# Start addresses of the weight tiles chosen by matmul width, and the gate block's low part of every second inner tile made by an adding transfer

## The chip, the cores and the metric

One core of one Trainium2 chip runs the whole program. The metric is device time in microseconds, lower is better; the time of a kernel is the median of its runs. A core has a matmul engine, TensorE (PE in the profile; its weight loads are PEld), three elementwise engines, VectorE (DVE), ScalarE (ACT) and GpSimd (POOL), and SyncE (SP), which here only issues transfers. GpSimd issues transfers too, among them the adding ones, whose data are added to what stands in SBUF.

## The reference

A two-layer streaming encoder on 512 frames of width 1024. Layer 0 mixes by an RWKV-7 scan, layer 1 by chunked attention; both attend to 256 memory tokens beside it, project, and end in a gated convolution block, which is where most of the change lies:

```python
def conv_glu(h, w_in, conv_w, conv_b, w_out):
    seq = h.shape[1]
    gate, val = jnp.split(h @ w_in, 2, axis=-1)          # 1024 -> 2 x 2816
    gp = jnp.pad(gate, ((0, 0), (CONV_W - 1, 0), (0, 0)))
    conv = conv_b + sum(conv_w[j] * gp[:, j:j + seq] for j in range(CONV_W))
    return (jax.nn.gelu(conv, approximate=False) * val) @ w_out

for layer in range(2):
    ...
    mo = memory_attention(q_mem, mem_n, w_mem_kv[layer])
    x = x + jnp.concatenate([mix, mo], axis=-1) @ w_out[layer]
    x = x + conv_glu(rms_norm(x, ln2[layer]), ffn_in[layer], ffn_conv[layer],
                     ffn_conv_b[layer], ffn_out[layer])
return rms_norm(x, ln_f)
```

## The kernel before

**Three matmuls for one product.** Each float32 operand is held as two parts of type float32r: a high part (a cast by ScalarE, `whi` for weights) and a low part (`wlo`, what the cast left off). A product is high by high, high by low and low by high. The low part of a weight tile comes in one of two ways: VectorE subtracts the high part from the raw weights, or ScalarE writes the negated raw weights and GpSimd issues an adding transfer that brings the weights in a second time. In that second way what is added in memory to minus the rounded copy is the weight, so the low part remains.

**Wide and narrow matmuls.** In the projections (`dense`, L221, L222, L225) the activations `r1h`, `r1l`, `r2h`, `r2l` are the moving operand, 512 columns at a time, and `whi` or `wlo` is loaded as 128x128 weights. In the output step of the gated block (`rows`, L658, L663) it is the other way round: slices of the activations are loaded and 512 columns of `whi` or `wlo` move. Both are called wide here. In the frames of the gated block (`prod`, L414, L416), and in the value projection of layer 1 (L1724 to L1726), 256 columns move: narrow.

**The frames.** The gated block's input product is done by seven block products in place of eight (Winograd's form of Strassen's scheme). There are 22 inner tiles of 128 columns (j). The tiles 0 to 20 are objects of the class `Seven`, one `frame` each, and tile 21 is done plainly in `ending`. A frame issues 7 calls of `prod`, each with 4 blocks of 3 matmuls: 84 narrow matmuls. Three calls use the normed activations (`XU`: r2h, r2l in layer 0, r1h, r1l in layer 1), four use sums of them (`XT`: th, tl in both layers). Weights of a frame are seven blocks of a raw tile, two raw tiles alternating: `load` fetches four (G1, V1, G2, V2), VectorE makes sums (`sums` L455, `sum2` L460, `sum4` L464). ScalarE casts four high parts a frame (`high`, L468), VectorE subtracts three low parts (`lower`, L473: two of 1024 columns, one of 512), and the low part of G2 and V2 comes by an adding transfer (`rest`, L450 and L451). The gate block G1 with S2 is the first operand of a frame (`gs`); its two parts are made in the frame before. Besides, VectorE and ScalarE end the tiles before (`end1` to `end5`), and GpSimd issues one adding transfer of the convolution (`endd`, L491). `keep` fixes the order of all of these on VectorE and ScalarE as it is written.

**Where tiles lie.** Tiles of the pool `wp` have 1024 words a partition. `whi` and `wlo` have three buffers each, in rotation. By the built program's allocations, in bytes from the start of a partition:

| tile | before | before, mod 128 | after | after, mod 128 |
|---|---|---|---|---|
| whi, three buffers | 66176, 70272, 74368 | 0 | 66560, 75008, 83456 plus 0 (wide) or 64 (narrow) | 0 or 64 |
| wlo, three buffers | 78464, 82560, 86656 | 0 | 70784, 79232, 87680 plus 128 (wide) or 64 (narrow) | 0 or 64 |
| r1h, r1l | 20640, 37024 | 32 | 20736, 37120 | 0 |
| r2h, r2l | 107136, 123520 | 0 | 108288, 124672 | 0 |
| th, tl | 152192, 168576 | 0 | 153344, 169728 | 0 |

Every operand of a wide or narrow matmul begins at a multiple of 512 bytes from its tile's start, so the last figure of a tile holds for all its slices. In what follows, the place of a matmul is the distance, mod 128 bytes, between the moving operand's start and the start of the weights that are loaded while it moves. Counted over the built order of float32r matmuls that follow one another (512 columns or 256):

| place | wide, before | wide, after | narrow, before | narrow, after |
|---|---|---|---|---|
| 0 | 1151 | 2256 | 2835 | 79 |
| 32 or 96 | 1140 | 36 | 1214 | 185 |
| 64 | 5 | 5 | 0 | 3785 |

Of the kernel before, what the change touches and what calls it, by code (L numbers as in the profile page):

```python
# [10 lines left out]
F32 = mybir.dt.float32  # L11
F32R = mybir.dt.float32r
AF = mybir.ActivationFunctionType
# [5 lines left out]
P = 128  # L19
S = 512  # L20
# [93 lines left out]


@with_exitstack
def trunk_kernel(ctx, tc, A, out):
# [19 lines left out]
    rc = cp.tile([P, 4], F32, name="rc")  # L137

# [32 lines left out]

    def split_w(raw, n, src=None, pin=lambda i: i, first=False, hold=False):
        hi = wp.tile([P, 1024], F32R, name="whi", tag="whi")
        lo = wp.tile([P, 1024], F32R, name="wlo", tag="wlo")
# [12 lines left out]
        if hold:  # L187
            return hi, lo, second
        second()
        return hi, lo  # L190

    def raw_w(src, n=1024):
        raw = wp.tile([P, 1024], F32, name="wraw", tag="wraw", bufs=2)
        raw_at[0] = nc.sync.dma_start(raw[:, :n], src)
        return raw[:, :n]

    def load_w(src, n=1024, lo=None):
        return split_w(raw_w(src, n), n, src if (lo_on[0] if lo is None else lo) else None)

# [30 lines left out]
    def run(g):  # L230
        for y in g:
            assert not callable(y) or y()
# [164 lines left out]
    def ffn(l, hp, U, T, new_x, xT, after=None, tokens=None):  # L397
# [22 lines left out]
        def keep(ins):  # L420
            return tc.keep_in_program_order(ins) if pinned[0] else ins
# [5 lines left out]
        class Seven:  # L427

            def __init__(self, j):
                self.j = j  # L430

# [34 lines left out]
            def high(self, what, n=1024):  # L466
                hi = wp.tile([P, 1024], F32R, name="whi", tag="whi")
                keep(SC.copy(hi[:, :n], self.pair(what) if n > S else self.raw[:, what]))  # L468
                return hi

            def lower(self, what, hi, n=1024):
                lo = wp.tile([P, 1024], F32R, name="wlo", tag="wlo")
                keep(V.tensor_tensor(lo[:, :n], self.pair(what) if n > S else self.raw[:, what], hi[:, :n], op=ALU.subtract))  # L473
                return hi, lo
# [31 lines left out]
            def frame(self, prev2, prev, nxt, norm=None, ending=None):  # L506
                first = prev is None
                if nxt:
                    nxt.load()
# [3 lines left out]
                if first:  # L513
                    hv = self.hv
                    self.h31 = self.high(S3)
                else:
                    hv = self.high(G2)
                keep(SC.copy(g[:, h1], f1[:, h1]))
                if first:
# [359 lines left out]
    def flat(t, n):  # L879

        return t[:].rearrange("p a b c -> p (a b c)").rearrange("p (m s) -> p m s", m=n)
# [4 lines left out]
    def lora_load(idx):  # L886
        raw = wp.tile([P, 1024], F32, name="wraw", tag="wraw", bufs=2)
        nc.sync.dma_start(raw[:], A["lora"][idx])
        return raw
# [5 lines left out]
    xs += [flat(kt_("AR", (P, NCH, 2, 64), bufs=2), 2) for _ in range(2)]  # L895
    lraw = wp.tile([P, 1024], F32, name="wraw", tag="wraw", bufs=2)
    for m in range(KD):
# [4 lines left out]
    nc.sync.dma_start(vec[:, 24:], A["vec"][:, 24:])  # L902
    kraw = wp.tile([P, 1024], F32, name="wraw", tag="wraw", bufs=2)
    nc.sync.dma_start(kraw[:], A["wA"][1])
# [16 lines left out]
    def lora_split(idx, raw, parts=1):  # L921

        hi, lo = zip(*((wp.tile([P, 1024], F32R, name="whi", tag="whi"), wp.tile([P, 1024], F32R, name="wlo", tag="wlo"))
                       for _ in range(2)))
        mraw = flat(kt_("KB", (P, NCH, 3, 64), bufs=2), 1)[:, 0, 0:1024]
        r3 = raw[:].rearrange("p (k f) -> p k f", k=8)
# [566 lines left out]
    def lora_one():  # L1493

        with tc.issue_after(norm_at[0].ins):
            *_, lw_ = lora_split(1, lora_load(1))
        yield from lora_pair(1, *lw_)


# [8 lines left out]
    GP.memset(acc[:, 0:S:64], 0.0)  # L1508
    run(lora0)
    first = prepare(0, Ts[0])  # L1510
    for _ in range(5):
# [131 lines left out]
    with ExitStack() as bctx:  # L1643
# [153 lines left out]
        run(dense(pk[:], [(wk, K8)], act1, order=K8[4:8], start=False))  # L1797
        wv = [load_w(A["w_kvv"][0, u]) for u in range(2)]
        run(norm)
# [189 lines left out]
```

## Time and profile before

| | us |
|---|---|
| median of 3 runs | 1302.26 (1301.45 to 1303.33) |
| profiled execution, its time | 1301.85 |
| profiled execution, its span | 1300.1 |
| ten steady frames of layer 0 (one matmul to the same matmul ten frames on) | 100.80 |
| ten steady frames of layer 1 | 100.00 |

The span is the time from the first to the last instruction; what lies around it is 1.75 us. The granted TensorE clock was 0.998 of full speed. In the profile's rows an engine, a line of the kernel, an operation, out<-in by tile names and a count stand first, then busy time and the mean duration of one. Matmuls overlap: a row of 283 ns each in a stream that starts one every 0.12 us means that the next starts long before the end of the last. Where all matmuls of a stream are alike, a difference between two rows' mean durations is a difference between their start-to-start times as well.

### The profile page before, as it was taken

To read this page: it belongs to the slowest core of one execution; us is meant where nothing else is said; L and a number is where in the kernel's file an instruction comes from. 1 tells how busy PE (TensorE), PEld (TensorE's weight loads), DVE (VectorE), ACT (ScalarE), POOL (GpSimd) and SP (SyncE) were. 2 spreads that over 40 slices of the span, in tenths; PEclk is the share of its full clock that TensorE was granted. 3 is DMA by queue.
4 is the path that set the end of the run, shared out by engine and by line. 5 is a ranking of instruction groups with operands and counts; after the bars stand their busy time and mean duration, and the time that the engine had idled before them with its cause. 6 is when DMAs were issued, how large, how long until landed. Compare 5 with 4: busy or idle time off the path is not lost.

```text
span 1300.1 us, 26329 instructions
## 1 busy us (share of the span) xinstructions
PE 1278.6 (98%) x10420; PEld 1100.9 (85%) x10420; DVE 1041.8 (80%) x1956; ACT 836.5 (64%) x1380; POOL 137.6 (11%) x164
## 2 busy tenths in 40 slices
PE   9999999999999999999999999999999999999997
PEld 7887777777789999999888878787799999998886
DVE  7967767775589999999876876658889999998684
ACT  6666767756566666767554676657757666665562
POOL 1000000000001112110220000000011122111200
PEclk9999999999999999999999999999999999999999
DMA  6365434452236777886984332223437878879951
GB/s 202 110 177 116 112 69 106 95 113 69 82 114 148 182 175 193 189 183 176 270 179 122 123 90 85 81 95 115 130 80 183 183 173 197 186 159 285 214 141 65
DMA packets 92988, 187.42 MB, mean 144 GB/s; under 512 B 21824, under 2 KB 30144, under 8 KB 92864
## 3 DMA queue, kind: packets, MB, share of 16 engines
q1 hardware_dynamic: 68592, 129.14, 31.1%
q0 software_dynamic: 24272, 56.59, 25.0%
q8 instruction: 82, 1.34, 0.4%
q14 instruction: 42, 0.34, 0.1%
HBM read 169.48 MB, written 6.29 MB: 135 GB/s over the span
## 4 chain that ended last, share of the span: by engine, by line
PE 83%; DVE 7%; ACT 6%; issue 1%; DMA 1%; SPq 0%; ACTq 0%; DVEq 0%
PE psf L414 21%; PE psf L416 11%; PE psf L658 7%; PE psd L225 6%; PE psd L221 6%; PE psd L222 5%; PE psf L663 4%; PE psd L658 3%; PE psd L663 2%; PE pss L1774 1%; PE pss L658 1%; DVE wlo L183 1%; PE pss L1404 1%; PE pss L350 1%; PE pss L1760 1%
## 5 line engine op out<-in xcount | busy, mean ns | idle before, releaser
L468 ACT CAST whi<-raw 128x1024 fp32r<-128x1024 f32 (+1 forms) x168 | 151.8, 941 | 66.2 <-PE psf L414 37.4
L414 PE MATMUL psf<-tl,whi 128*128 128x256 f32 x672 | 168.6, 283 | 0.0
L414 PE MATMUL psf<-th,whi 128*128 128x256 f32 x672 | 168.3, 283 | 0.0
L473 DVE TENSOR_TENSOR wlo<-raw,whi 128x1024 fp32r<-128x1024 f32 (+1 forms) x126 | 131.5, 1043 | 14.3 <-ACT whi L468 14.2
L175 ACT CAST whi<-wraw 128x1024 fp32r<-128x1024 f32 x84 | 87.7, 1047 | 69.3 <-PE psd L222 36.1
L414 PEld LDWEIGHTS psf<-tl,whi 128*128 128x128 f32 x672 | 128.7, 192 | 0.0
L414 PEld LDWEIGHTS psf<-th,whi 128*128 128x128 f32 x672 | 128.5, 192 | 0.0
L221 PE MATMUL psd<-r1h,whi 128*128 128x512 f32 x264 | 108.2, 410 | 0.0
L222 PE MATMUL psd<-r1l,whi 128*128 128x512 f32 x264 | 105.6, 401 | 0.0
L183 DVE TENSOR_TENSOR wlo<-wraw,whi 128x1024 fp32r<-128x1024 f32 x65 | 79.3, 1219 | 15.9 <-ACT whi L175 13.6
L648 ACT CAST whi<-raw 128x1024 fp32r<-128x1024 f32 (+1 forms) x52 | 49.6, 954 | 65.2 <-PE psf L658 35.4
L649 DVE TENSOR_TENSOR wlo<-raw,whi 128x1024 fp32r<-128x1024 f32 (+1 forms) x52 | 56.7, 1099 | 42.6 <-ACT whi L648 33.6
L416 PE MATMUL psf<-th,wlo 128*128 128x256 f32 x504 | 81.2, 283 | 0.0
L225 PE MATMUL psd<-r1h,wlo 128*128 128x512 f32 x264 | 74.9, 405 | 0.0
L416 PEld LDWEIGHTS psf<-th,wlo 128*128 128x128 f32 x504 | 69.7, 192 | 0.0
L451 POOL DMA_DIRECT2D wlv<-in_ffn_in_dram x40 | 61.2, 1530 | 59.7 <-DVE tmp L535 58.7
L494 ACT ACTIVATE tmp<-tmp,vec 128x512 f32<-128x512 f32 x44 | 35.9, 817 | 47.3 <-DVE tmp L481 47.1
L414 PE MATMUL psf<-r2h,whi 128*128 128x256 f32 x252 | 63.3, 283 | 0.5 <-ACT whi L468 0.5
L414 PE MATMUL psf<-r2l,whi 128*128 128x256 f32 x252 | 63.2, 283 | 0.0
L414 PE MATMUL psf<-r1h,whi 128*128 128x256 f32 x252 | 62.5, 281 | 0.5 <-ACT whi L468 0.5
L414 PE MATMUL psf<-r1l,whi 128*128 128x256 f32 x252 | 62.1, 279 | 0.0
L221 PEld LDWEIGHTS psd<-r1h,whi 128*128 128x128 f32 x264 | 49.5, 188 | 13.0 <-issue 2.5
(608 smaller groups left out, 3545.7 us busy)
## 6 DMA issues: line engine op xcount, KB each, us to landing
raw<-in_ffn_in_dram SPq DMA_DIRECT2D x42, 512.0 KB, 3.8
raw<-in_ffn_in_dram SPq DMA_DIRECT2D x84, 256.0 KB, 4.2
wlv<-in_ffn_in_dram POOLq DMA_DIRECT2D x40, 512.0 KB, 8.0
raw<-in_ffn_out_dram SPq DMA_DIRECT2D x30, 512.0 KB, 5.9
raw<-in_ffn_out_dram POOLq DMA_DIRECT2D x24, 512.0 KB, 8.0
wraw<-in_wA_dram SPq DMA_DIRECT2D x20, 512.0 KB, 4.2
wraw<-in_w_out_dram SPq DMA_DIRECT2D x16, 512.0 KB, 3.9
wraw<-in_ffn_outp_dram SPq DMA_DIRECT2D x16, 512.0 KB, 4.7
```

The costliest lines, as they stand in the source:

```text
L175: high = lambda: pin(SC.copy(hi[:, :n], raw))
L183: pin(V.tensor_tensor(lo[:, :n], raw, hi[:, :n], op=ALU.subtract))
L221: PE.matmul(ps, wh[:, j * P:(j + 1) * P], ah, start=start and n == 0, stop=False)
L222: dense_at[0] = PE.matmul(ps, wh[:, j * P:(j + 1) * P], al, start=False, stop=False)
L225: dense_at[0] = PE.matmul(ps, wl[:, j * P:(j + 1) * P], act(k)[0], start=False, stop=stop and n == len(ks) - 1)
L414: PE.matmul(ps, wh[:, o + k * P:o + k * P + P], x[k][n], start=k == n == 0, stop=False)
L416: PE.matmul(ps, wl[:, ol + k * P:ol + k * P + P], x[k][0], start=False, stop=k == 3)
L451: GP.dma_start(self.low[:].rearrange("p (a s) -> p a s", a=2), self.second, accum_op=ALU.add)
L468: keep(SC.copy(hi[:, :n], self.pair(what) if n > S else self.raw[:, what]))
L473: keep(V.tensor_tensor(lo[:, :n], self.pair(what) if n > S else self.raw[:, what], hi[:, :n], op=ALU.subtract))
L658: PE.matmul(ps[:], a[:, k0 + i, ts], hi[:, i * S:i * S + S], start=bool(first) and (first is True or t in first) and a is act[0] and i == ...
L663: PE.matmul(ps[:], act[0][:, k0 + i, ts], lo[:, i * S:i * S + S], start=False, stop=bool(last) and t in last and i == n - 1)
```

## The change

It has four parts.

1. **Places by width.** Tiles of `wp` get 1056 words and a tag for each slot; the 1024 words used start at word 0 (`whi`) or 32 (`wlo`) for wide use, and at word 16 for narrow use. Two small tiles are padded, so that `r1h` and all behind it move.
2. **Slots by hand.** `wtile` takes slots in rotation, passes over those in `held` (the two pairs of the first projections), and lets the frames name the slot of `wlo`: S3 has slot 0, S4 and the gate block have slot 1 or 2 by the parity of j.
3. **The gate block of j = 2, 4, ... 18** (`APART`) gets the low part of its first half by `rest1`: ScalarE writes minus the raw block (512 columns) and GpSimd issues an adding transfer of 256 KB, early in the frame before. `both` then subtracts the other half (S2) alone on VectorE: 512 columns in place of 1024.
4. **Loads written earlier.** `load` for tile j+2 is written behind the low part of S4 of frame j; before, it stood at the start of frame j+1.

```diff
+W_AT = {"whi": 0, "wlo": 32}
+W_NARROW = 16
+APART = range(2, 20, 2)
...
+    turns, held = {"whi": 0, "wlo": 0}, set()
+    def wtile(name, dt=F32R, tag=None, at=None, slot=None):
+        if name in turns:
+            n = turns[name] if slot is None else slot
+            while (name, n) in held:
+                n = (n + 1) % 3
+            turns[name] = (n + 1) % 3
+            tag = f"{name}{n}"
+            at = W_AT[name] if at is None else at
+        else:
+            at = at or 0
+        t = wp.tile([P, 1056], dt, name=name, tag=tag or name, bufs=1 if name in turns else 2)
+        return t[:, at:at + 1024]
...
-    vec = cp.tile([P, NVEC], F32, name="vec")
+    vec = cp.tile([P, NVEC + 28], F32, name="vec")[:, :NVEC]
...
-                self.low = wp.tile([P, 1024], F32R, name="wlv", tag="wraw", bufs=2)
+                self.low = wtile("wlv", tag="wraw", at=W_NARROW)
...
+            def rest1(self):
+                self.slot = 1 + self.j % 2
+                self.low1 = wtile("wlo", at=W_NARROW, slot=self.slot)
+                keep(SC.activation(self.low1[:, :S], self.raw[:, G1], AF.Copy, scale=-1.0))
+                GP.dma_start(self.low1[:, :S], A["ffn_in"][l, self.j, 0][:, 0:S], accum_op=ALU.add)
+
+            def both(self):
+                hi = self.high(G1)
+                keep(V.tensor_tensor(self.low1[:, S:2 * S], self.raw[:, S2], hi[:, S:2 * S], op=ALU.subtract))
+                self.gs = hi, self.low1
...
             def frame(self, prev2, prev, nxt, norm=None, ending=None):
                 first = prev is None
-                if nxt:
+                if first:
                     nxt.load()
...
                     hv = self.high(G2)
+                if nxt and nxt.apart:
+                    nxt.rest1()
                 keep(SC.copy(g[:, h1], f1[:, h1]))
...
                 w4 = self.lower(S4, self.high(S4, S), S)
+                if self.j + 2 < NFF - 1:
+                    made[self.j + 2].load()
...
                 if nxt:
-                    nxt.gs = nxt.lower(G1, nxt.high(G1))
+                    if nxt.apart:
+                        nxt.both()
+                    else:
+                        nxt.gs = nxt.lower(G1, nxt.high(G1))
                     nxt.sum4()
...
-                hi = wp.tile([P, 1024], F32R, name="whi", tag="whi")[:, :n * S]
-                lo = wp.tile([P, 1024], F32R, name="wlo", tag="wlo")[:, :n * S]
+                hi = wtile("whi")[:, :n * S]
+                lo = wtile("wlo")[:, :n * S]
...
+        held.update((n_, (turns[n_] + 1 + i_) % 3) for n_ in turns for i_ in range(2))
...
-            wv = wv or [load_w(A["w_kvv"][g, u]) for u in range(2)]
+            wv = wv or [load_w(A["w_kvv"][g, u], at=W_NARROW) for u in range(2)]
```

ScalarE, where frame 1 of layer 0 follows frame 0 (`rho` and `g` are copies out of PSUM; the three casts are the gate block, S3 and G2). Before:

```order
L450 ACTIVATE wlv<-raw 128x1024
L468 CAST whi<-raw 128x1024 x3
L305 COPY rho<-pss 128x512
L518 COPY tmp<-psf 128x256
L468 CAST whi<-raw 128x512
```

After:

```order
L470 ACTIVATE wlv<-raw 128x1024
L499 CAST whi<-raw 128x1024 x3
L476 ACTIVATE wlo<-raw 128x512
L553 COPY tmp<-psf 128x256
L325 COPY rho<-pss 128x512
```

The negated block of tile 2 stands between the three casts and the copy of `f1`, and the copy of `rho` has fallen behind that one.

VectorE, from the second sum of tile 2 in frame 1 of layer 0 to the end of `g` at the start of frame 2. Before:

```order
L460 TENSOR_TENSOR raw<-raw 128x512
L548 TENSOR_TENSOR tmp<-psf,tmp 128x256
L473 TENSOR_TENSOR wlo<-raw,whi 128x1024
L464 TENSOR_TENSOR raw<-raw 128x512
L561 TENSOR_TENSOR tmp<-tmp,psf 128x512
L563 TENSOR_TENSOR tmp<-tmp,psf 128x256
```

After:

```order
L491 TENSOR_TENSOR raw<-raw 128x512
L585 TENSOR_TENSOR tmp<-psf,tmp 128x256
L481 TENSOR_TENSOR wlo<-raw,whi 128x512
L495 TENSOR_TENSOR raw<-raw 128x512
L601 TENSOR_TENSOR tmp<-tmp,psf 128x512
L603 TENSOR_TENSOR tmp<-tmp,psf 128x256
```

The gate block's subtraction (L473 before, L481 after) has half its columns; nothing else on VectorE moved in the frames.

GpSimd, from frame 0 of layer 0 on (`wlv` is the low part of G2 and V2, `tmp<-r1h` the convolution's transfer). Before:

```order
L451 DMA wlv<-in_ffn_in_dram 128x2x512
L491 DMA tmp<-r1h 128x510
L451 DMA wlv<-in_ffn_in_dram 128x2x512
L491 DMA tmp<-r1l 128x510
L451 DMA wlv<-in_ffn_in_dram 128x2x512
```

After:

```order
L471 DMA wlv<-in_ffn_in_dram 128x2x512
L477 DMA wlo<-in_ffn_in_dram 128x512
L522 DMA tmp<-r1h 128x510
L471 DMA wlv<-in_ffn_in_dram 128x2x512
L522 DMA tmp<-r1l 128x510
```

In every second frame one transfer more stands ahead of the two that were there. SyncE's rows of the frames (L435, L437 before; L455, L457 after) stand in the same order in both.

In layer 0's first projections the slots passed over let the scheduler move rows. TensorE there, before (`psl<-ML` belongs to the memory keys):

```order
L222 MATMUL psd<-r1l,whi 128x512
L221 MATMUL psd<-r1h,whi 128x512
L222 MATMUL psd<-r1l,whi 128x512
L221 MATMUL psl<-ML,whi 128x256
L222 MATMUL psl<-ML,whi 128x256
```

After, at the same row:

```order
L242 MATMUL psd<-r1l,whi 128x512
L241 MATMUL psd<-r1h,whi 128x512
L242 MATMUL psd<-r1l,whi 128x512
L241 MATMUL psd<-r1h,whi 128x512
L241 MATMUL psl<-ML,whi 128x256
```

The projection of r1h goes on for seven rows where the memory keys cut in before; those seven stood some 35 rows further on.

More of the change, by code (lines that the diff above doesn't have):

```diff
@@ L136, in trunk_kernel @@
     rho = cp.tile([P, S], F32, name="rho")
-    rc = cp.tile([P, 4], F32, name="rc")
+    rc = cp.tile([P, 12], F32, name="rc")[:, :4]
     def C(name, lo=0, n=None):
@@ L170, in trunk_kernel, with split_w @@
     raw_at = [None]
-    def split_w(raw, n, src=None, pin=lambda i: i, first=False, hold=False):
-        hi = wp.tile([P, 1024], F32R, name="whi", tag="whi")
-        lo = wp.tile([P, 1024], F32R, name="wlo", tag="wlo")
+    def split_w(raw, n, src=None, pin=lambda i: i, first=False, hold=False, at=None):
+        hi = wtile("whi", at=at)
+        lo = wtile("wlo", at=at)
         high = lambda: pin(SC.copy(hi[:, :n], raw))
@@ L192, in raw_w, with load_w @@
     def raw_w(src, n=1024):
-        raw = wp.tile([P, 1024], F32, name="wraw", tag="wraw", bufs=2)
+        raw = wtile("wraw", F32)
         raw_at[0] = nc.sync.dma_start(raw[:, :n], src)
         return raw[:, :n]
-    def load_w(src, n=1024, lo=None):
-        return split_w(raw_w(src, n), n, src if (lo_on[0] if lo is None else lo) else None)
+    def load_w(src, n=1024, lo=None, at=None):
+        return split_w(raw_w(src, n), n, src if (lo_on[0] if lo is None else lo) else None, at=at)
     def mm3(ps, wh, wl, ah, al, start, stop):
@@ L429, in __init__ @@
             def __init__(self, j):
-                self.j = j
+                self.j, self.slot, self.apart = j, 1 + j % 2, j in APART
             def load(self):
@@ L466, in high @@
             def high(self, what, n=1024):
-                hi = wp.tile([P, 1024], F32R, name="whi", tag="whi")
+                hi = wtile("whi", at=W_NARROW)
                 keep(SC.copy(hi[:, :n], self.pair(what) if n > S else self.raw[:, what]))
@@ L471, in lower @@
             def lower(self, what, hi, n=1024):
-                lo = wp.tile([P, 1024], F32R, name="wlo", tag="wlo")
+                lo = wtile("wlo", at=W_NARROW, slot={S3: 0, S4: self.slot, G1: self.slot}[what])
                 keep(V.tensor_tensor(lo[:, :n], self.pair(what) if n > S else self.raw[:, what], hi[:, :n], op=ALU.subtract))
@@ L514, in frame @@
                     hv = self.hv
+                    turns["whi"] = (turns["whi"] + 1) % 3
                     self.h31 = self.high(S3)
+                    turns["whi"] = (turns["whi"] + 1) % 3
                 else:
                     hv = self.high(G2)
+                if nxt and nxt.apart:
+                    nxt.rest1()
                 keep(SC.copy(g[:, h1], f1[:, h1]))
@@ L886, in lora_load @@
     def lora_load(idx):
-        raw = wp.tile([P, 1024], F32, name="wraw", tag="wraw", bufs=2)
+        raw = wtile("wraw", F32)
         nc.sync.dma_start(raw[:], A["lora"][idx])
@@ L895, in trunk_kernel @@
     xs += [flat(kt_("AR", (P, NCH, 2, 64), bufs=2), 2) for _ in range(2)]
-    lraw = wp.tile([P, 1024], F32, name="wraw", tag="wraw", bufs=2)
+    lraw = wtile("wraw", F32)
     for m in range(KD):
@@ L902, in trunk_kernel @@
     nc.sync.dma_start(vec[:, 24:], A["vec"][:, 24:])
-    kraw = wp.tile([P, 1024], F32, name="wraw", tag="wraw", bufs=2)
+    kraw = wtile("wraw", F32)
     nc.sync.dma_start(kraw[:], A["wA"][1])
@@ L921, in lora_split @@
     def lora_split(idx, raw, parts=1):
-        hi, lo = zip(*((wp.tile([P, 1024], F32R, name="whi", tag="whi"), wp.tile([P, 1024], F32R, name="wlo", tag="wlo"))
+        hi, lo = zip(*((wtile("whi"), wtile("wlo"))
                        for _ in range(2)))
+        held.update((n_, (turns[n_] + 1 + i_) % 3) for n_ in turns for i_ in range(2))
         mraw = flat(kt_("KB", (P, NCH, 3, 64), bufs=2), 1)[:, 0, 0:1024]
@@ L1497, in lora_one @@
         yield from lora_pair(1, *lw_)
+        held.clear()
     lora0 = lora_pair(0, *lw)
@@ L1509, in trunk_kernel @@
     run(lora0)
+    held.clear()
     first = prepare(0, Ts[0])
@@ L1797, in trunk_kernel @@
         run(dense(pk[:], [(wk, K8)], act1, order=K8[4:8], start=False))
-        wv = [load_w(A["w_kvv"][0, u]) for u in range(2)]
+        wv = [load_w(A["w_kvv"][0, u], at=W_NARROW) for u in range(2)]
         run(norm)
```

## The prediction

> **What bounds the kernel now.** I read the page first, then stretches of time, then single rows.
>
> ```profile
> PE 1278.6 (98%) x10420; PEld 1100.9 (85%) x10420; DVE 1041.8 (80%) x1956; ACT 836.5 (64%) x1380; POOL 137.6 (11%) x164
> PE 83%; DVE 7%; ACT 6%; issue 1%; DMA 1%; SPq 0%; ACTq 0%; DVEq 0%
> ```
>
> TensorE is busy nearly throughout and carries 83% of the chain that ended last. So what counts is how fast its stream can start matmuls, and whether something else keeps it from that. The stretches (columns: time, then PE, PEld, DVE, ACT and POOL busy):
>
> ```profile
> 20.00:345.00 325.00, 317.93 (x4269) 246.43 (x4268) 236.76 (x654) 212.24 (x425) 15.74 (x20) 1.00 0.43 103
> 345.00:385.00 40.00, 40.00 (x172) 31.54 (x171) 31.50 (x48) 25.25 (x36) 1.75 (x2) 1.00 0.50 158
> 441.24:542.04 100.80, 100.80 (x842) 100.80 (x841) 97.03 (x142) 69.56 (x92) 21.46 (x20) 1.00 0.80 186
> 740.00:920.00 180.00, 176.04 (x1018) 138.39 (x1017) 121.36 (x324) 119.81 (x280) 1.69 (x9) 1.00 0.29 91
> 1045.82:1145.82 100.00, 100.00 (x842) 100.00 (x841) 96.18 (x141) 68.82 (x92) 21.49 (x20) 1.00 0.81 185
> 1176.00:1240.00 64.00, 64.00 (x278) 52.01 (x277) 48.59 (x47) 35.86 (x44) 13.91 (x16) 1.00 0.98 258
> ```
>
> In the frames (third and fifth row) TensorE never pauses, and VectorE is at 96%. Also gapless are the output projection of layer 0 (second) and the output step of layer 1's gated block (last). In the two mixers it pauses here and there.
>
> Frame lengths, from the same matmul in frames ten apart (layer 0, then layer 1):
>
> ```profile
> 452.17 0.64 PE L416 MATMUL psf<-r2h,wlo 128*128 128x256 f32 x4
> ...
> 552.97 0.64 PE L416 MATMUL psf<-r2h,wlo 128*128 128x256 f32 x4
> ...
> 1046.78 0.52 PE L416 MATMUL psf<-r1h,wlo 128*128 128x256 f32 x3
> ...
> 1146.78 0.52 PE L416 MATMUL psf<-r1h,wlo 128*128 128x256 f32 x3
> ```
>
> Layer 0: 10.08 us a frame, 120.0 ns for each of 84 matmuls. Layer 1: 10.00 us, with the same 84. VectorE's first sum in the same frames, ten apart:
>
> ```profile
> 447.52 1.22 DVE L455 TENSOR_TENSOR raw<-raw 128x1024 f32<-128x1024 f32 x1
> ...
> 547.12 1.22 DVE L455 TENSOR_TENSOR raw<-raw 128x1024 f32<-128x1024 f32 x1
> ...
> 1051.99 1.22 DVE L455 TENSOR_TENSOR raw<-raw 128x1024 f32<-128x1024 f32 x1
> ...
> 1151.64 1.22 DVE L455 TENSOR_TENSOR raw<-raw 128x1024 f32<-128x1024 f32 x1
> ```
>
> VectorE moves on by 9.96 us a frame in both layers, whatever TensorE does: it starts late and gains on it, 0.12 us a frame in layer 0 and 0.04 in layer 1. So TensorE sets the frames, and VectorE's own round of 9.96 us lies just below. Any gain of TensorE past 9.96 us needs a shorter round there.
>
> **Part 1, places: the wide matmuls.** Rows of gapless stretches; the first two stand at place 0, the others at 32 or 96:
>
> ```profile
> L658 PE MATMUL psf<-whi,th 128*128 128x512 f32 x32 | 12.5, 389 | 0.0
> L225 PE MATMUL psd<-r2h,wlo 128*128 128x512 f32 x30 | 7.6, 389 | 0.0
> ...
> L658 PE MATMUL psd<-whi,r1h 128*128 128x512 f32 x28 | 7.2, 395 | 0.0
> L225 PE MATMUL psd<-r1h,wlo 128*128 128x512 f32 x40 | 10.5, 395 | 0.0
> ```
>
> Same line, width and engine: 389 ns at place 0, 395 at the others. After the change nearly all of the 1140 unequal wide matmuls stand at 0. By the built order 189 of them lie in layer 0's output projection, 248 in layer 1's output step and 48 in its tile 21: 485 by 6 ns, 2.9 us, and these stretches are gapless, so that counts whole. The other 655 lie in the mixers: at most 3.9 us, at least none, where chains between engines pace TensorE:
>
> ```profile
> L221 PE MATMUL psd<-r1h,whi 128*128 128x512 f32 x205 | 84.8, 414 | 0.0
> PE pss L1334 <- ACT Y L1323: 1.3, 5, 0.3
> ```
>
> Their mean of 414 ns shows that much stands between them, but the longest total of waits there is 1.3 us and TensorE is 98% busy, so I take a little over half, 2.1 us. Wide in all: 5.0 us (2.9 to 6.8).
>
> **Part 1, places: the narrow matmuls.** Frames of layer 1 hold both places, side by side:
>
> ```profile
> L414 PE MATMUL psf<-th,whi 128*128 128x256 f32 x176 | 44.1, 283 | 0.0
> L414 PE MATMUL psf<-r1h,whi 128*128 128x256 f32 x133 | 32.9, 280 | 0.0
> ...
> L221 PE MATMUL psl<-ML,whi 128*128 128x256 f32 x32 | 8.1, 289 | 0.6 <-ACT vm L1024 0.6
> L222 PE MATMUL psl<-ML,whi 128*128 128x256 f32 x32 | 7.9, 281 | 0.0
> ```
>
> Place 0 (th) 283 ns, place 32 (r1h) 280; the last two are from layer 0's mixer, place 96, with a wait in the first. Narrow matmuls thus want the opposite of wide ones. The 36 that use r1h and r1l make the frame 0.08 us shorter: 2.2 ns each, 117.8 for 120.0. After the change all stand at 64, where no float32r narrow matmul stood. The nearest rows are streams at 64 in front of the transposes of layer 1, whose weights are plain float32:
>
> ```profile
> 844.38 0.28 PE L1726 MATMUL psd<-wlo,r1h 128*128 128x256 f32 x1
> 844.50 0.60 PE L1760 MATMUL pss<-cst,sb 128*128 128x128 f32 x4
> ...
> 865.67 0.40 PE L222 MATMUL psd<-r2l,whi 128*128 128x512 f32 x1
> 865.90 0.60 PE L1760 MATMUL pss<-cst,sb 128*128 128x128 f32 x4
> ```
>
> The narrow stream takes 0.12 us, which leaves it open; the wide one 0.23, as at 32 and 96 and not as at 0 (389 - 395 + 0.233 us would be 0.227). So 64 is not another 0, and behaves like its neighbours. I take 117.8. The low end: the four transposes of 128 columns in the second row start 0.107 us apart ((0.60 - 0.28) / 3), so a start every 107 ns cannot be excluded, but VectorE's round then binds (below). The high end: 123, since the slowest narrow rows, L221 and L222 on ML, have 285 ns in the mean, 2 above place 0, and a nanosecond for what none shows.
>
> At 117.8 a frame takes 9.895 us. Layer 0: 21 frames by 0.185, 3.9 us. Layer 1: 48 matmuls at 2.2, 0.106 a frame, 2.2 us. Together 6.1 (the transposes and value projection stay).
>
> The Trainium skill speaks against all of part 1: "TensorE: Matmul & The Clock Gate", section "Step-by-step: what each phase is for", says that TensorE reads moving operand and weights by two independent ports, so that loading weights takes nothing from a running matmul. By that no place matters. The rows of 389 and 395 ns do not agree with it; its result is the third rival.
>
> **Part 3, the adding transfer.** Prices on VectorE and elsewhere:
>
> ```profile
> L473 DVE TENSOR_TENSOR wlo<-raw,whi 128x1024 fp32r<-128x1024 f32 x36 | 44.0, 1222 | 5.3 <-ACT whi L468 5.3
> L473 DVE TENSOR_TENSOR wlo<-raw,whi 128x512 fp32r<-128x512 f32 x18 | 12.3, 685 | 0.0
> L445 ACT ACTIVATE tmp<-raw x4: 615/617/617, 365.0 to 930.8; 128x512 fp32r<-128x512 f32 x4
> L446 POOL DMA_DIRECT2D tmp<-in_ffn_in_dram x4: 859/886/1209, 365.9 to 931.7; - x4
> DMA to landing us min/median/max: 3.8/4.5/5.0
> ```
>
> VectorE: 1222 - 685 = 0.537 us less in every second frame. The wait of 0.3 us for the gate block's cast stays. Its round becomes 9.43 and 9.96 in turn, 9.695 in the mean, below TensorE's 9.895. So this part is what lets part 1 go below 9.96; by itself it buys nothing in the frames, since TensorE sets them.
>
> ScalarE gets 0.617 us nine times a layer, in front of the copy of `f1`. It is 69% busy, and has half a microsecond of slack just there:
>
> ```profile
> 440.63 1.99 ACT L468 CAST whi<-raw 128x1024 fp32r<-128x1024 f32 x2
> ...
> 443.77 0.62 ACT L468 CAST whi<-raw 128x512 fp32r<-128x512 f32 x1 [0.51 <-PE psf L414]
> ```
>
> GpSimd then issues at about 443.3 (casts to 442.6, 0.6 more), 0.9 us, and by the same kind of transfer (256 KB, L446) it lands 4.5 us later, at 448. Its first reader is the low product of the next frame at 452.17: 4 us of cover, and if it took as long as the 512 KB one (about 8 us), it would land just in time. Two transfers of GpSimd follow it in the frame, but not before 448:
>
> ```profile
> 448.15 0.91 POOL L491 DMA_DIRECT2D tmp<-r1h  x1 [7.80 <-ACT r1h L484]
> ```
>
> so nothing queues behind it there. The added traffic is 256 KB against about 1.8 MB a frame; the DMA share goes from 0.8 to some 0.9. A new demand: the raw gate block must have landed by the time of the third cast, an early one.
>
> ```profile
> 447.02 0.94 SPq L437 DMA_DIRECT2D raw<-in_ffn_in_dram  x2
> raw<-in_ffn_in_dram SPq DMA_DIRECT2D x32, 256.0 KB, 4.2
> ```
>
> Issued to 447.96 it lands near 452, and the negated copy would start near 452.6. If it is late by up to half a microsecond more, ScalarE's slack hides it. I count nothing.
>
> **Parts 2 and 4.** Loads: SyncE has nothing else to issue in the frames and its order stays, so they start when the raw buffer is free, as before: nothing. The slots: in the frames S4 takes the gate block's slot, whose readers end 24 matmuls into the frame, before S4's subtraction: nothing. At the start of layer 0 the order changes for some 20 us of work; bound plus or minus 2 us by TensorE's pauses of the first 80 us, no sign known: nothing.
>
> Sum: 5.0 + 6.1 = 11.1 us off 1301.85, 1290.75. The profiled execution is 0.4 us below the median of 1302.26, so about 1291. Differences under 0.2% (2.6 us) cannot be told from none.
>
> **Rivals.** *Place 64 is much cheaper than 32.* From 115.4 ns on VectorE's 9.695 us binds, whatever TensorE could do. Layer 0 then gains 0.385 a frame, 8.1 us, layer 1 0.305, 6.4: with 5.0 wide, 19.5 in all, 1283. For it: 32 already helps, and nothing shows that the gain peaks there. Against: the wide rows at 64 equal those at 32.
>
> *Narrow at 64 is as at 0.* Layer 0 gains nothing, layer 1 loses 0.08 a frame, 1.7 us; with the wide gain of 5.0, 1299. For it: the row of 0.12 us.
>
> *Places decide nothing,* and 283 against 280 has another cause in layer 1. Then the frames stay at 10.08 and 10.00, VectorE's relief lies under TensorE: 1302. Against: both widths, in two stretches each, split by place alone.
>
> *Narrow at 64 is dearer than at 0* (slower). Each nanosecond over 120 costs 3.5 us on 3528 matmuls, beside the 1.7 of layer 1; the wide gain is used up at 120.9 ns, and from there the kernel is slower. At 123 it takes about 1309. For it: no float32r pair at this place is in the trace. Against: the streams of 0.12 us at 64, and that all three unequal places cost the same when wide.
>
> **Chances.** My forecast (place 64 within a nanosecond or so of 32) 0.50; much cheaper 0.25; like 0, 0.13; nothing 0.06; dearer 0.06. The range 1281 to 1299 takes the first two whole and part of the third, with the 2 us of the start. Faster: 0.50 + 0.25 + 0.12 = 0.87; same: 0.08, the rest of the third and the fourth; slower 0.05.
>
> **What would show it.** The wide groups on r1h at 389 ns; the narrow groups of all frames alike, at 281 or so; frames of 9.9 us in both layers with no wait of TensorE; VectorE's L481 at 685 ns and its round at 9.7. Wrong would be: narrow groups at 283, a frame that alternates in length (VectorE binds), or TensorE waiting for `wlo` from a transfer.

## The result, and the profile after

| | before | after |
|---|---|---|
| median, us (same chip, 5 runs each) | 1303.05 (1301.45 to 1303.48) | 1292.25 (1291.13 to 1294.4) |
| profiled execution: time, span | 1301.85, 1300.1 | 1294.4, 1292.6 |

The ratio is 0.9921 (95% interval 0.991 to 0.9932): 10.8 us off, where 11.1 were forecast. The profiled execution after is the longest of its five, 2.15 us over the median. So the two traces differ by 7.5 us, the medians by 10.8.

The page of the kernel after, engines and chain:

```profile
PE 1260.9 (98%) x10420; PEld 1083.1 (84%) x10420; DVE 1031.7 (80%) x1956; ACT 846.4 (65%) x1398; POOL 152.7 (12%) x182
PE 62%; DVE 15%; ACT 8%; DMA 8%; issue 6%; SPq 0%; POOL 0%; ACTq 0%; DVEq 0%; POOLq 0%
```

TensorE's share of the chain fell from 83% to 62%, and transfers have 8% of it where they had 1%. The frames and layer 1's output step, as stretches of time (the columns of the prediction):

```profile
441.24:542.04 100.80, 100.36 (x876) 99.74 (x875) 96.95 (x146) 73.54 (x99) 25.75 (x25) 1.00 0.91 204
1045.82:1145.82 100.00, 98.08 (x857) 97.49 (x857) 95.42 (x143) 73.78 (x98) 25.34 (x25) 1.00 0.89 198
1176.00:1240.00 64.00, 64.00 (x287) 52.94 (x287) 51.00 (x50) 38.01 (x49) 13.87 (x16) 1.00 0.95 236
```

TensorE now pauses in the frames. VectorE is still at 96% of its time (95% in layer 1), though one subtraction in every second frame has half the columns: the frames follow faster on one another. The DMA share rose from 0.80 to 0.9. Groups of layer 1's frames, and one of the output step:

```profile
L434 PE MATMUL psf<-th,whi 128*128 128x256 f32 x279 | 67.0, 277 | 0.5 <-ACT tmp L553 0.5
L434 PE MATMUL psf<-r1h,whi 128*128 128x256 f32 x204 | 48.9, 276 | 0.0
L436 PE MATMUL psf<-th,wlv 128*128 128x256 f32 x68 | 11.1, 286 | 3.5 <-DMA wlv<-in_ffn_in_dram 3.5
...
L698 PE MATMUL psd<-whi,r1h 128*128 128x512 f32 x28 | 7.0, 389 | 0.0
```

The wide group on r1h went from 395 to 389 ns, as forecast. The narrow ones went from 283 and 280 to 276, where 281 was forecast; the row on `wlv` holds waits. TensorE's longest waits in all:

```profile
PE psf L436 <- DMA wlv<-in_ffn_in_dram: 4.1, 7, 1.6
PE psf L434 <- ACT whi L499: 2.0, 3, 0.7
PE psf L434 <- ACT tmp L553: 1.9, 5, 0.6
...
PE psd L245 <- DMA wlo<-in_ffn_in_dram: 1.0, 2, 0.5
```

The first, third and fourth of these (line numbers of after: L553 is the copy of `f1`, L245 the low products of `dense`) were absent from the trace of before. The narrow price, from four low matmuls of one frame in a row, and VectorE's first sum ten frames apart:

```profile
540.24 0.62 PE L436 MATMUL psf<-r2h,wlo 128*128 128x256 f32 x4
...
448.37 1.22 DVE L486 TENSOR_TENSOR raw<-raw 128x1024 f32<-128x1024 f32 x1
...
545.04 1.22 DVE L486 TENSOR_TENSOR raw<-raw 128x1024 f32<-128x1024 f32 x1
```

Before, such a four took 0.64 us. Now (0.62 - 0.28) / 3 is 0.113 us from start to start, and the shortest frames take 9.52 us, 84 by 113.3 ns. VectorE moves on by 9.67 us a frame in the mean, 9.37 and 9.97 in turn. It, and not TensorE, is now the slower of the two. Its round is not all work: in every frame with an adding transfer it waits 0.33 us for ScalarE's cast of the gate block (5.9 us before 18 subtractions at L481).

Stages, from the first and last frame matmuls and the last of each output step in the two traces (us):

| stage | before | after | difference |
|---|---|---|---|
| start to layer 0's frames | 388.4 | 387.6 | -0.7 |
| frames 0 to 20, layer 0 | 213.9 | 210.2 | -3.7 |
| tile 21 and output step | 124.3 | 125.7 | +1.3 |
| mixer of layer 1 | 226.4 | 225.8 | -0.5 |
| frames 0 to 20, layer 1 | 212.6 | 209.5 | -3.2 |
| tile 21 and output step | 126.7 | 126.1 | -0.6 |

Two things stand out: an output step that got longer, and layer 0's frame 0, which went from 11.89 to 14.65 us. For the latter, VectorE's rows around the last output-projection block, before:

```profile
378.03 1.22 DVE L183 TENSOR_TENSOR wlo<-wraw,whi 128x1024 fp32r<-128x1024 f32 x1
...
388.58 0.69 DVE L387 TENSOR_TENSOR xT<-xT,psd 128x512 f32<-128x512 f32 x1 [2.18 <-PE psd L225]
```

and after, with TensorE's row between them:

```profile
387.56 1.22 DVE L203 TENSOR_TENSOR wlo<-wraw,whi 128x1024 fp32r<-128x1024 f32 x1
388.83 2.11 PE L245 MATMUL psd<-r1h,wlo 128*128 128x512 f32 x8
...
390.98 0.69 DVE L407 TENSOR_TENSOR xT<-xT,psd 128x512 f32<-128x512 f32 x1 [2.21 <-PE psd L245]
```

That block's low part is made 9.5 us later, its low products run behind ten matmuls of frame 0, and the last tile of x, on which the whole normed operand hangs, is 2.4 us late. The slots told why: `made[0]` names slot 1 of `wlo`, the rotation goes on from there, and the block gets slot 2, which the block before it still occupies.

### The profile page after: what moved, and what is told of

Its sections match the earlier page's. It is cut to its first block, busy times and chain, and to the rows that moved or that the text cites. A ratio compares the mean times of both kernels' runs of the same rounds, so it can differ in the third digit from the quotient of the medians.

```text
span 1292.6 us, 26432 instructions
## 1 busy us (share of the span) xinstructions
PE 1260.9 (98%) x10420; PEld 1083.1 (84%) x10420; DVE 1031.7 (80%) x1956; ACT 846.4 (65%) x1398; POOL 152.7 (12%) x182
## 4 chain that ended last, share of the span: by engine, by line
PE 62%; DVE 15%; ACT 8%; DMA 8%; issue 6%; SPq 0%; POOL 0%; ACTq 0%; DVEq 0%; POOLq 0%
PE psf L434 8%; PE psf L698 7%; PE psd L245 6%; PE psd L241 5%; PE psd L242 5%; DMA wlv<-in_ffn_in_dram 4%; PE psf L436 4%; PE psf L703 4%; PE psd L698 3%; ACT whi L499 2%; DMA wraw<-in_ffn_in_dram 2%; PE psd L703 2%; DVE raw L486 1%; PE pss L1817 1%; DVE wlo L504 1%
## 5 line engine op out<-in xcount | busy, mean ns | idle before, releaser
L434 PE MATMUL psf<-th,whi 128*128 128x256 f32 x672 | 161.4, 278 | 2.5 <-ACT tmp L553 1.9
L434 PE MATMUL psf<-tl,whi 128*128 128x256 f32 x672 | 161.1, 276 | 0.0
L434 PEld LDWEIGHTS psf<-th,whi 128*128 128x128 f32 x672 | 125.8, 188 | 3.9 <-ACT tmp L553 2.9
L434 PEld LDWEIGHTS psf<-tl,whi 128*128 128x128 f32 x672 | 126.0, 188 | 0.0
L504 DVE TENSOR_TENSOR wlo<-raw,whi 128x1024 fp32r<-128x1024 f32 (+1 forms) x108 | 109.3, 1012 | 9.1 <-ACT whi L499 8.9
L689 DVE TENSOR_TENSOR wlo<-raw,whi 128x1024 fp32r<-128x1024 f32 (+1 forms) x52 | 56.5, 1097 | 38.9 <-ACT whi L688 31.5
L436 PE MATMUL psf<-th,wlo 128*128 128x256 f32 x504 | 78.0, 276 | 0.0
L245 PE MATMUL psd<-r1h,wlo 128*128 128x512 f32 x264 | 74.3, 403 | 0.6 <-DMA wlo<-in_ffn_in_dram 0.4
L436 PEld LDWEIGHTS psf<-th,wlo 128*128 128x128 f32 x504 | 66.8, 188 | 0.0
```

The source lines that it names most:

```text
L245: dense_at[0] = PE.matmul(ps, wl[:, j * P:(j + 1) * P], act(k)[0], start=False, stop=stop and n == len(ks) - 1)
L434: PE.matmul(ps, wh[:, o + k * P:o + k * P + P], x[k][n], start=k == n == 0, stop=False)
L436: PE.matmul(ps, wl[:, ol + k * P:ol + k * P + P], x[k][0], start=False, stop=k == 3)
```

## Experiments

All medians below were taken beside the kernel before, whose median was 1302.66 to 1303.12 us on these chips.

**slot_back.** In the kernel after:

```diff
+                if l == 0 and m == KD - 1:
+                    turns["wlo"] = 0
                 w = load_w(A["w_out"][l, m])
```

> One line is added to the changed kernel: the last output-projection block of layer 0 takes low-part slot 0 instead of slot 2, which the block before it still uses. Theory (the hand-made slots delay that block's low part until its forerunner has been read, and so the last x tile and frame 0 by 2.4 us): frame 0 of layer 0 falls from 14.65 to about 11.9 us, the last sum of xT (L407) comes 2.2 to 2.4 us earlier, and the whole takes 1289.5 to 1290.5 us. Rival (frame 0 is long because its tiles' transfers or casts are late anyway): frame 0 stays above 14 us and the whole within 0.5 us of 1292.25.

1290.7 us (1289.72 to 1291.32), ratio 0.9904 (0.9891 to 0.9917). Frame 0 took 11.82 us. VectorE's rows:

```profile
376.08 2.36 DVE L203 TENSOR_TENSOR wlo<-wraw,whi 128x1024 fp32r<-128x1024 f32 x2
...
388.19 0.69 DVE L409 TENSOR_TENSOR xT<-xT,psd 128x512 f32<-128x512 f32 x1 [1.81 <-PE psd L245]
```

The low part is made at 377, and the last sum ends 2.8 us earlier. The slots were the cause. The median gained 1.55 us of it (2.2 by the ratios, whose intervals overlap a little); frame 1 of its trace gave 1.5 us back (12.07 us, where after had 10.60).

**no_adding.** `APART = ()`.

> The changed kernel with the list of tiles for the adding transfer empty: every gate block is split on VectorE, places, slots and early loads stay. Theory A (VectorE's round of 9.96 us binds once TensorE's floor is 9.52): frames of 9.96 us in both layers, no wait of TensorE for wlv, the whole about 4 us slower, 1296. Theory B (what keeps the frames from 9.52 is the added traffic and not VectorE): frames come down to 9.5 to 9.7 and the whole to 1280 to 1286.

1300.87 us (1300.04 to 1302.29), ratio 0.9984 (0.9976 to 0.9993). VectorE, ten frames apart, and the stretch:

```profile
428.61 1.22 DVE L486 TENSOR_TENSOR raw<-raw 128x1024 f32<-128x1024 f32 x1
...
528.26 1.22 DVE L486 TENSOR_TENSOR raw<-raw 128x1024 f32<-128x1024 f32 x1
...
441.24:542.04 100.80, 99.54 (x849) 97.52 (x848) 96.68 (x142) 69.67 (x92) 21.56 (x21) 1.00 0.80 187
```

9.965 us a frame, VectorE's old round, and TensorE's frames had it too (9.96 to 9.98 in about half of them, 10.00 in the mean from frame 2 on). Theory A held; the loss, 8.6 us, was twice what I expected. So all the places together, with frame 0's loss and without VectorE's relief, buy 2 us; the relief makes it 8.6 more.

**every_tile.** `APART = range(2, 20)`.

> The changed kernel with the adding transfer for each of the tiles 2 to 19 instead of every second: VectorE's own round falls to 9.43 us in each frame, and the traffic of a frame rises by 256 KB in the other half of the frames. Theory B (transfers bound the frames): waits for wlv grow, frames of 9.9 to 10.3 us, the whole 1294 to 1302. Theory A (VectorE is what holds the frames above TensorE's 9.52): frames of 9.5 to 9.6 us, the whole 1281 to 1284.

1303.61 us (1299.49 to 1307.99), ratio 1.0002 (0.9989 to 1.0014).

```profile
441.24:542.04 100.80, 97.74 (x853) 96.81 (x852) 92.08 (x143) 74.67 (x101) 31.12 (x32) 1.00 0.97 213
...
PE psf L434 <- ACT tmp L553: 13.9, 20, 1.7
```

Theory B: VectorE has room (91%), the transfer engines are at 0.97, frames take 10.2 and 10.03 us. TensorE waits for the copy of `f1`, and that stands on ScalarE behind `rest1`, which waits for the raw block (40.9 us in all, before 31 of its 36 copies). The time is 1.6 us over the range expected for it. Both theories are true, each on its side: VectorE sets the frames with no adding transfer, the transfers with one for every tile.

**narrow_32** and **narrow_0.** `W_NARROW = 8` and `W_NARROW = 0`.

> The changed kernel with the narrow weights at place 32 instead of 64, all else equal; this is the price on which the prediction's sum stood. By the rows of before a narrow matmul starts every 117.8 ns and a frame takes at least 9.895 us. If the frames are then TensorE's, both layers have frames of 9.9 us with few waits, and the whole takes 1292.25 + 20 x (9.90 - 9.80) = 1294 us, 1.7 us over the changed kernel. Rival (in the changed kernel the frames are set by transfers and VectorE, so that the place counts for nothing): 1292 to 1292.5. If waits add to the 9.895, 1296 or more.

> The changed kernel with the narrow weights at place 0. A narrow matmul starts every 120.0 ns by the rows of before: frames of 10.08 us in both layers, no wait for wlv or for the copy of f1 after the first frames (in 10.08 us the transfers keep up), the gate's low part taken off VectorE to no use. Against narrow_32 (frames of 9.92, 1300.37) 40 x 0.16 = 6.4 us more: 1306 to 1307, slower than before, with frame 0's loss in it. Rival (the place acts only through something else): within 1 us of narrow_32.

1300.37 us (1298.33 to 1303.59), ratio 0.9984 (0.9975 to 0.9993), and 1302.21 us (1300.61 to 1305.58), ratio 0.9995 (0.9986 to 1.0004). The same matmul in frames ten apart, narrow_32:

```profile
490.96 0.64 PE L436 MATMUL psf<-r2h,wlo 128*128 128x256 f32 x4
...
590.16 0.64 PE L436 MATMUL psf<-r2h,wlo 128*128 128x256 f32 x4
```

and narrow_0:

```profile
441.53 0.63 PE L436 MATMUL psf<-r2h,wlo 128*128 128x256 f32 x4
...
541.53 0.63 PE L436 MATMUL psf<-r2h,wlo 128*128 128x256 f32 x4
```

Frames of 9.92 and 10.00 us, without stalls behind the first six. The frame at 32 is what the prediction took (9.895); narrow_0's 10.08 was 0.08 too long. But narrow_32's total missed its 1294 by 6 us. In its trace layer 0's frames take 214.8 us in all, longer than before's 213.9: frame 0 costs 14.68, frames 1 and 5 10.95 and 10.68, and the other 18 save 0.16 each. So place 64 against 32 is worth 8 us here, and at the price I had forecast the change would have brought 2.7 us and not 11.

The cheap place is not every narrow matmul's. In the value projection of layer 1 the weight tile moves and the activations are loaded, the other way round than in the frames. It stands at 64 as well after the change, and hardly moved (before, then after):

```profile
L1726 PE MATMUL psd<-wlo,r1h 128*128 128x256 f32 x64 | 17.8, 281 | 0.0
...
L1769 PE MATMUL psd<-wlo,r1h 128*128 128x256 f32 x64 | 17.7, 279 | 0.0
```

From start to start its narrow matmuls take 118.2 ns before, 117.8 after, and 118.2 in narrow_32 and in narrow_0.

**wide_32.** `W_AT = {"whi": 8, "wlo": 24}`.

> The changed kernel with the weights of the wide matmuls 32 bytes off, so that nearly all 2300 wide matmuls stand at place 32 or 96; the narrow ones stay at 64. It is twice the number that the change moved (1140), since those that stood at 0 before move too. If the price of 5 to 6 ns lay fully on the path: 2300 x 5.5 = 12.6 us, 1305. If as my sum had it, a little under three quarters: 9 us, 1301. If chains between engines hide most of it outside the gapless stretches: 2 to 5 us, 1294 to 1297.

1300.3 us (1299.07 to 1303.28), ratio 0.9981 (0.9972 to 0.999): 8 us over the kernel after, 3.5 ns for each of 2300 matmuls. One group of the output step, which stood at place 0 (389 ns) before the change and after it:

```profile
L698 PE MATMUL psf<-whi,th 128*128 128x512 f32 x26 | 10.3, 396 | 0.0
```

By stages (traces): the two output steps 2.8 and 3.8 us longer, the mixer of layer 1 1.2, the first stage none. The output steps pay the price in full, the mixers hardly. My 9 us was near. This run prices all 2300 places; the change moved only 1140 of them, and of layer 0's output step, which pays here, none.

**wide_before.** `vec` and `rc` without the padding, so that r1h and r1l lie 32 bytes off again.

> The changed kernel without the 28 and 8 words of padding behind vec and rc, so that r1h and r1l, and with them the 1140 wide matmuls, stand 32 bytes off again as before; the narrow ones stay at 64, but for the 36 a frame on r1h and r1l in layer 1 (now at 96). By the prediction's sum the wide places are worth 5.0 us (2.9 to 6.8): 1297.2 (1295 to 1299). By the stages of the two traces (mixer of layer 1 and last output step 0.5 us each, first stage 0.7) 1.8 us: 1294. The 36 matmuls make layer 1's frames 9.72 at least, against VectorE's 9.695: under 1 us of it.

1295.46 us (1294.15 to 1296.16), ratio 0.9942 (0.9929 to 0.9954). Against the kernel after: 3.2 us by the medians, 2.7 by the ratios, and up to half a microsecond of it is layer 1's frames, whose shortest are 9.71. The wide places are worth about 2.7 us, not 5.0; with the two intervals it can be anything from 0.6 to 4.8.

**apart_only.** As wide_before, and `W_NARROW = 0`.

> The changed kernel with all places as they were before (no padding, narrow weights at 0), so only the adding transfer, the loads a frame ahead and the hand-made slots. As predicted, the adding transfer buys nothing while TensorE sets the frames: frames of 10.08 and 10.00 us without waits. With frame 0's loss of 2 to 2.7 us by the slots: 1304.5 to 1306, slower than before. Rival (VectorE's relief is worth something by itself): 1300 or less.

1303.32 us (1302.95 to 1305.21), ratio 1.0007 (0.9997 to 1.0016): no gain from the adding transfer alone, as predicted. Not slower either: layer 0's steady frames came out at 10.00, not 10.08, which gives back 1.4 us of the 3.1 that frames 0 and 1 lost in the trace. (So its places are not quite those of before; more on this at the end.)

**copy_first** and **gate_first**, both on slot_back. The first moves `rest1` behind the cast of S4:

```diff
-                if nxt and nxt.apart:
-                    nxt.rest1()
                 keep(SC.copy(g[:, h1], f1[:, h1]))
...
                 w4 = self.lower(S4, self.high(S4, S), S)
+                if nxt and nxt.apart:
+                    nxt.rest1()
```

> slot_back (1290.7 us) with one move: the gate block's negated copy and its adding transfer (rest1) are issued behind the copy of f1 and the cast of S4 on ScalarE, and no longer ahead of them. Theory (rest1 waits for the raw block's landing and holds up the copy of f1, which shows as 3.5 us of TensorE waiting for ScalarE's L553 in slot_back): that wait goes to under 0.5 us, the whole 1287 to 1289.5. Rival (the low part, issued about 2 us later, then lands too late, or the next transfer queues behind it): waits for wlo or more waits for wlv, the whole 1291 to 1295.

1299.79 us (1297.06 to 1302.03), ratio 0.9975 (0.9966 to 0.9984): 9 us worse, more than the rival had.

```profile
PE psf L436 <- DMA wlo<-in_ffn_in_dram: 7.5, 8, 2.0
PE psf L436 <- DMA wlv<-in_ffn_in_dram: 3.5, 6, 1.4
```

The wait for the copy of `f1` is gone, and the low part itself is late. The frames of the other tiles stay at 9.52 us, those of the tiles with the adding transfer stall at their first low product (the longest took 13.41), or at that on `wlv`. The transfer had less slack than the 4 us I had read. In the longest frame the granted clock fell too: it was 0.81 in the mean of 1095 to 1104 us, and behind a wait of 2.2 us some 15 matmuls started 213 ns apart, 1.6 us in all. Whether the wait brought that about, this run doesn't show.

The second loads the gate block first:

```diff
+                nc.sync.dma_start(self.raw[:, G1], A["ffn_in"][l, self.j, 0][:, 0:S])
                 nc.sync.dma_start(self.raw[:, G2:V2 + 1], self.second)
-                for o, a in ((V1, 1), (G1, 0)):
-                    nc.sync.dma_start(self.raw[:, o], A["ffn_in"][l, self.j, a][:, 0:S])
+                nc.sync.dma_start(self.raw[:, V1], A["ffn_in"][l, self.j, 1][:, 0:S])
```

> slot_back (1290.7 us) with another order of a tile's three raw loads: the gate block first, then the pair of 512 KB, then V1, so that rest1 needs only the first to have landed. Theory as for copy_first: the waits for ScalarE's L553 (3.5 us) go to under 0.5 us, and the whole to 1287 to 1289.5. Rival (the transfer engines are near their rate, 200 GB/s and busy 0.90 of the time, so that what lands earlier makes another land later): waits for wlv or for VectorE's sums in their place, the whole 1290 to 1292.

1288.81 us (1288.59 to 1289.81), ratio 0.9894 (0.9879 to 0.9909). No wait for the copy of `f1` is left among the longest; waits and VectorE's round:

```profile
PE psf L436 <- DMA wlv<-in_ffn_in_dram: 2.4, 5, 0.9
PE psd L245 <- DMA wlo<-in_ffn_in_dram: 1.6, 2, 0.9
...
426.24 1.22 DVE L486 TENSOR_TENSOR raw<-raw 128x1024 f32<-128x1024 f32 x1
...
522.92 1.22 DVE L486 TENSOR_TENSOR raw<-raw 128x1024 f32<-128x1024 f32 x1
```

Frames of 9.76 us in the mean of 1 to 19, against VectorE's 9.67. Against slot_back it is 1.9 us by the medians and 1.3 by the ratios, whose intervals overlap; that the wait of 3.5 us for the copy of `f1` is gone is the firmer sign.

**every_third.** gate_first with `APART = range(2, 20, 3)`.

> gate_first with the adding transfer for every third tile instead of every second. VectorE's round is 9.78 us in the mean instead of 9.695, the traffic of a frame 1.92 MB instead of 1.965. If in gate_first VectorE's round sets the frames (9.76 in the mean there): frames of 9.80 to 9.85, 1290.5 to 1292. If the transfers still set them: frames of 9.70 or less, 1286.5 or less.

1293.12 us (1292.33 to 1294.13), ratio 0.9924 (0.9912 to 0.9936): 4.3 us slower than gate_first with less traffic. VectorE, nine frames apart:

```profile
436.40 1.22 DVE L486 TENSOR_TENSOR raw<-raw 128x1024 f32<-128x1024 f32 x1
...
524.30 1.22 DVE L486 TENSOR_TENSOR raw<-raw 128x1024 f32<-128x1024 f32 x1
```

9.77 us a frame, and frames of 9.82. VectorE sets them: 0.1 us more a frame is the 4 us. It is a microsecond over the range expected, and on the side of this theory.

**own_subtraction**, on gate_first: tile 21's gate block without an adding transfer.

```diff
-            wg = split_w(raw_w(src[0]), 1024, src[0], keep, True, True)
+            wg = split_w(raw_w(src[0]), 1024, None, keep, hold=True)
             yield
-            wg[2]()
...
             made[j - 2].end4()
+            wg[2]()
```

> gate_first (1288.8 us) with tile 21's gate block split by VectorE instead of by an adding transfer, the subtraction put where VectorE has no next tile to serve. Theory (the faster frames bring TensorE to tile 21 before that transfer has landed, 1.6 us of waiting for wlo in gate_first, none before the change): that wait goes, 1287.0 to 1287.6. Rival (the output step is paced by its own blocks and casts, so the wait moves on): 1288.5 to 1289, or slower where the subtraction holds up VectorE.

1286.13 us (1285.53 to 1286.51), ratio 0.987 (0.9857 to 0.9884), the fastest version, and about a microsecond better than expected. The wait for `wlo` is gone; the output steps take 124.3 and 124.9 us, where gate_first had 125.9 and 126.6. What remains is

```profile
PE psf L436 <- DMA wlv<-in_ffn_in_dram: 3.4, 7, 0.8
```

## Why the prediction was right, and where its steps were not

The time was right and the direction too, but not by the case that I gave the highest chance. That the gain came out within 0.3 us of the sum is luck: two errors of opposite sign met.

- **Places, narrow: the step that failed.** "So 64 is not another 0, and behaves like its neighbours" carried a finding on wide matmuls over to narrow ones. In the frames, narrow at 64 costs 113.3 ns and not 117.8. The row I had called undecided (0.12 us) could not tell: it ends the value projection, which stays at 118 ns at every place tried. The transposes' 0.107 us was nearer to the truth than the rows I preferred.
- **So the first rival's mechanism held**: VectorE binds. VectorE's round was forecast at 9.43 and 9.96 in turn, mean 9.695; it is 9.37 and 9.97, mean 9.67. no_adding and every_third show it from both sides. What I named as a sign against me, a frame that alternates, is there, on VectorE.
- **Why 1292 and not the rival's 1283.** Wide places brought 2.7 us where 5.0 stood (2.3); frame 0 lost 2.8 in the trace and layer 0's output step 1.3; frames 1 to 19 take 9.80 and 9.91 us in the profiled execution and not 9.695 (6.1), of which 2.15 is that execution's distance to the median. 1283 + 2.3 + 2.8 + 1.3 + 6.1 - 2.15 is 1293.4, close to the 1292.25 measured. This is an account drawn from one trace, not an experiment: that the 2.15 lies in the frames is assumed, and mending frame 0 brought the median less than its 2.8. With frame 0, the gate block's landing and tile 21 mended, own_subtraction stands at 1286. So the two errors are a narrow price read too high, and losses that I had not counted.
- **Wide: mis-sized, 5.0 for 2.7.** The price of 6 ns was right, and the result lies near the lower bound of 2.9. What was sized too high is above all the 2.1 us for the mixers. The first stage took 385.7 to 389.5 us in all kernels, with no order by place: the mixer of layer 0 hides the price. And of the 1.5 us of layer 1's output step only 0.6 was left: tile 21's adding transfer, whose landing no wait showed before, now comes too late. Without it (own_subtraction) both output steps are 1.6 us shorter than in gate_first, more than the waits that the trace names (1.6 us in all); where the rest comes from is open.
- **Adding transfer: two counts right, one wrong.** VectorE's `low1` subtraction takes 0.69 us as forecast, and the transfer lands in 4.4 us (4.5 forecast). That it buys nothing by itself is shown by apart_only, which has the early loads and the slots in it as well. That the traffic costs nothing was wrong: raw blocks of 256 KB land in 5.5 us (4.2 before) and `wlv` in 8.6 (8.0). ScalarE's half microsecond of slack didn't cover a raw gate block that late: it waited for it before 9 of its 18 negated copies, 6.7 us in all. Loading it first was worth 1.9 us by the medians.
- **Parts 2 and 4, counted at nothing.** The loads can't be told apart in these runs; that part alone wasn't tried. The slots were not nothing: I asked only when readers in the frames end, and not what the rotation hands to the next block of the output projection.
- **Places decide nothing**: excluded by narrow_32, wide_32 and wide_before. The Trainium skill, "TensorE: Matmul & The Clock Gate", section "Step-by-step: what each phase is for", with its two independent read ports, does not describe this: the same matmuls differ by 8 us in total when the weights are moved by 32 bytes.
- **Narrow like 0**: narrow_0 gives 1302, 3 more than that rival's 1299, with the same losses in it (its frame 0 takes 14.70 us). **Dearer than 0**: not so.

## What to carry to other kernels

When an engine is made faster, its next bound is already in the profile as another engine's own round; read that, and ask of each handover (a low part, a raw block, the last tile) whether it still arrives in time. A finding on operand places holds for the width that showed it, and for which operand moves and which is loaded, and no further. Where rotating buffers get a fixed slot, follow the rotation past the place where the slot is named.

## What was not expected of the hardware

Start-to-start times of float32r matmuls, by the distance mod 128 bytes between the moving operand and the weights loaded meanwhile, in streams of these runs: 256 columns in the frames 119.8 to 120.0 ns at 0 (before), about 118 at 32 and 96 (before and narrow_32), 113.6 to 114.2 at 64 (means with short stalls in them); 512 columns 228 at 0 and 233 at 32 and 96. The distance is not the whole of it. The value projection's 256 columns take 117.8 at 64. And in narrow_0 and apart_only, at 0, layer 0's matmuls between two low ones on `wlo` take 116.0 in the mean, those on `wlv` 118 and most others 120.0: 15 in a frame by 4 ns and 6 by 2 are most of the 0.08 us by which these frames fall short of 10.08. By the addresses the tiles of `wlo` are 128 mod 256 bytes from the moving activations in these two runs, and 0 before. But the last high matmul ahead of the low ones, at the same distance to them, takes 120.0. So what sets this is open.

An adding transfer costs the transfer engines nearly twice a plain one. Queues in layer 0's frames of the kernel after (413 to 588 us; megabytes, share of 16 engines):

```profile
q0 software_dynamic: 8755, 16.44, 55.7%
q1 hardware_dynamic: 9588, 17.94, 32.5%
```

q0 has the adding ones, q1 the plain loads that SyncE issues: 16.44 MB in 0.557 of 175 us is 169 GB/s over the time that the packets took, against 315 for the plain loads of q1. A frame with an adding transfer for each tile has 1.05 MB of plain and 1.05 MB of adding traffic, 3.3 + 6.2 = 9.5 us of all engines: that fits every_tile, whose frames of 10.0 to 10.2 us had the engines 0.97 busy at 213 GB/s. The Trainium skill, "DMA: Bandwidth & Descriptors", section "Measured (HBM→SBUF, 128 partitions, SWDGE, issued from GpSimd)", has 341 GB/s for 1 MB of a load that GpSimd issues. The plain queue's 315 here is near it; the adding one's 169 has no row in that table.
